# Top-2 gating scale: the second group's loads move to the scalar queue, in four parts

## The chip, the cores and the metric

The kernel runs on one core of a Trainium2 chip. The metric is the device time of one execution in microseconds (us).

## The reference

For 16 x 1024 = 16,384 tokens of 512 floats, `x` holds the tokens and `router_logits` eight logits a token. The two largest of the eight softmax probabilities are divided by their sum, and the token is written out twice, once scaled by each:

```python
probs = np.exp(router_logits - logits_max)
probs = probs / np.sum(probs, axis=-1, keepdims=True)
topk_indices = np.argsort(probs, axis=-1)[..., -k:]
topk_probs = np.take_along_axis(probs, topk_indices, axis=-1)
topk_probs = topk_probs / np.sum(topk_probs, axis=-1, keepdims=True)
x_expanded = x[:, :, np.newaxis, :].repeat(k, axis=2)
return (x_expanded * topk_probs[..., np.newaxis])
```

So 34 MB are read and 67 MB are written, and the arithmetic is one multiplication for each output element.

## The kernel before

Each of the 128 partitions handles 128 tokens ("rows"), in two groups of 65 and 63. A row is 2 KB when it is loaded and 4 KB when it is stored. The buffer `xs` has room for 65 loaded rows, `osp` for 18 output rows (of 4 KB), `WA` holds the two weights of every row.

The first group's rows are loaded in three transfers on the sync queue (6, 28 and 31 rows; line 120). The logits follow the first of them (lines 125 and 126), and `top2_weights` works out all weights: maxima and minima on VectorE, two sigmoids on ScalarE.

Then each of nine blocks is multiplied on VectorE (line 133), from `xs` into either `osp` or a part of `xs` whose rows have been used up, and stored by one transfer (line 145). The blocks, called stores 1 to 9, have 3, 15, 16, 15 and 16 rows in the first group and 16, 16, 15 and 16 in the second. Store 1 is issued on the scalar queue, all others on the sync queue. Two blocks that go into `osp` again (stores 4 and 8) are multiplied in two pieces: the first 3 (or 2) rows early, the others when an earlier store has left that part of `osp`.

The second group's rows come in three loads (16, 16 and 31 rows) that are issued on the sync queue behind store 5. The first two go into rows of `xs` that held store 3's output, the third into rows that held store 5's output, so they wait until those stores have landed.

All transfers of one queue are worked off in the order in which they are issued. Each engine's instructions, and each queue's issues, run in the order of the program; the waits between engines follow from the buffers' rows.

Of the kernel before, what the change touches and what calls it, by code (L numbers as in the profile page):

```python
# [1 line left out]

# [4 lines left out]

F32 = mybir.dt.float32
ALU = mybir.AluOpType
ACTF = mybir.ActivationFunctionType  # L10
P = 128


def top2_weights(nc, WA, dlt, room, logits, E):

    tt = nc.vector.tensor_tensor
    hi, lo, n = None, None, E  # L20
    while n > 1:
        n //= 2
        if hi is None:
            a, b = logits[:, :, 0:n], logits[:, :, n : 2 * n]
            nhi, nlo = room(n), b
            tt(nhi, a, b, op=ALU.max)  # L26
            tt(nlo, a, b, op=ALU.min)  # L27
        else:
            a, b = hi[:, :, 0:n], hi[:, :, n : 2 * n]
            nhi, nlo, tmp = room(n), room(n), room(n)  # L30
            tt(tmp, lo[:, :, 0:n], lo[:, :, n : 2 * n], op=ALU.max)  # L31
            tt(nlo, a, b, op=ALU.min)  # L32
            tt(nlo, nlo, tmp, op=ALU.max)  # L33
            tt(nhi, a, b, op=ALU.max)  # L34
        hi, lo = nhi, nlo
    tt(dlt, hi[:, :, 0], lo[:, :, 0], op=ALU.subtract)  # L36
    nc.scalar.activation(WA[:, :, 0], dlt, ACTF.Sigmoid, scale=-1.0)  # L37
    nc.scalar.activation(WA[:, :, 1], dlt, ACTF.Sigmoid, scale=1.0)  # L38

GROUPS = [65, 63]

LOADS = [[6, 28, 31], [16, 16, 31]]
BASE = [0, 1]

STORES = [
    [(0, 3, "osp", 0), (3, 15, "osp", 3), (18, 16, "xs", 0), (34, 15, "osp", 0), (49, 16, "xs", 33)],
    [(0, 16, "osp", 2), (16, 16, "xs", 0), (32, 15, "osp", 0), (47, 16, "xs", 32)],
]  # L50

L = 18

FREE = [3, 2]


@with_exitstack
def kernel(
    ctx: ExitStack,
    tc: tile.TileContext,  # L60
    x: bass.AP,
    router_logits: bass.AP,
    k: bass.AP,
    out: bass.AP,
):
    nc = tc.nc
    B, S, D = x.shape
    E = router_logits.shape[-1]
    N = B * S
    assert int(k) == 2 and E == 8 and N == P * sum(GROUPS)  # L70
    M = N // P

    x_v, o_v, rl_v = [], [], []
    t0 = 0
    for n in GROUPS:
        t1 = t0 + P * n
        x_v.append(
            x.rearrange("b s d -> (b s) d")[t0:t1].rearrange("(p m) d -> p m d", p=P)
        )
        o_v.append(  # L80
            out.rearrange("b s k d -> (b s) k d")[t0:t1].rearrange(
                "(p m) k d -> p m k d", p=P
            )
        )
        rl_v.append(
            router_logits.rearrange("b s e -> (b s) e")[t0:t1].rearrange(
                "(p m) e -> p m e", p=P
            )
        )
        t0 = t1  # L90

    wpool = ctx.enter_context(tc.tile_pool(name="wpool", bufs=1))
    xs = wpool.tile([P, max(GROUPS), D], F32)
    osp = wpool.tile([P, L, 2, D], F32)
    WA = wpool.tile([P, M, 2], F32)
    dlt = wpool.tile([P, M], F32)


    flat = osp.rearrange("p l k d -> p (l k d)")
    taken = [0]  # L100

    def room(n):
        o = taken[0]
        taken[0] += M * n
        return flat[:, o : o + M * n].rearrange("p (m n) -> p m n", n=n)

    logits = room(E)

    def place(where, at, n):

        if where == "osp":
            return osp[:, at : at + n]
        return xs[:, at : at + 2 * n, :].rearrange("p (r k) d -> p r k d", k=2)

    m0 = 0
    for g, G in enumerate(GROUPS):
        x0, r = BASE[g], 0
        for n in LOADS[g]:
            tc.keep_in_program_order(
                nc.sync.dma_start(xs[:, x0 + r : x0 + r + n, :], x_v[g][:, r : r + n, :])  # L120
            )
            r += n
            if g == 0 and r == 6:
                n0 = GROUPS[0]
                tc.keep_in_program_order(nc.sync.dma_start(logits[:, :n0], rl_v[0]))  # L125
                tc.keep_in_program_order(nc.sync.dma_start(logits[:, n0:], rl_v[1]))  # L126
                top2_weights(nc, WA, dlt, room, logits, E)
        assert r == G
        for r, n, where, at in STORES[g]:
            og = place(where, at, n)  # L130
            again = where == "osp" and at == 0 and r > 0
            for a, b in [(0, FREE[g]), (FREE[g], n)] if again else [(0, n)]:
                nc.vector.tensor_tensor(  # L133
                    og[:, a:b],
                    xs[:, x0 + r + a : x0 + r + b, :]
                    .unsqueeze(2)
                    .to_broadcast([P, b - a, 2, D]),
                    WA[:, m0 + r + a : m0 + r + b, :]
                    .unsqueeze(3)
                    .to_broadcast([P, b - a, 2, D]),  # L140
                    op=ALU.mult,
                )

            queue = nc.scalar if g == r == 0 else nc.sync
            tc.keep_in_program_order(queue.dma_start(o_v[g][:, r : r + n], og))  # L145
        m0 += G


# [1 line left out]
_INS = ['x', 'router_logits', 'k']  # L150
_OUTS = [((16, 1024, 2, 512), 'float32')]

_NUMBERS = {'k': 2}


# [26 lines left out]
```

## Time and profile before

| | |
|---|---|
| median of 3 runs | 239.9 us (239.83 to 239.99) |
| the profiled execution | 239.92 us |
| its span in the profile | 238.1 us |
| VectorE busy | 141.9 us (60% of the span) |
| ScalarE busy | 1.8 us |
| DMA | 101.19 MB in 2448 packets, mean 425 GB/s |

The span is what the profile shows between the first and the last instruction; the execution's own time is 1.8 us longer. An instruction that issues a transfer (SPq for the sync queue, ACTq for the scalar queue) takes 0.3 to 0.5 us, and the transfer runs on the 16 DMA engines after that. "To landing" is the time from the issue to the moment at which all 16 engines have reported the transfer complete; it holds the time for which the transfer stood behind others.

### The profile page before, as it was taken

What the parts mean: (1) busy time and instruction counts of PE and PEld (TensorE: products, weight loads), DVE (VectorE), ACT (ScalarE), POOL (GpSimd) and SP (SyncE); (2) the same over time, 40 slices, a digit from 0 to 9 for tenths busy, and PEclk for the clock granted to TensorE, in tenths of its full rate; (3) what the DMA queues carried; (4) which work ended last, traced back from release to release, by engine and by line L of the source; (5) the groups of instructions that cost most, each with busy time, mean ns of one, the idle gap of its engine ahead of it and who ended that gap; (6) DMA issues with size and microseconds to landing.
All of it is one profiled execution on the core that took longest, in us unless ns stands there. A gap on an engine that the chain in (4) does not pass through costs nothing.

```text
span 238.1 us, 102 instructions
## 1 busy us (share of the span) xinstructions
DVE 141.9 (60%) x22; ACT 1.8 (1%) x3; POOL 0.2 (0%) x4
## 2 busy tenths in 40 slices
DVE  0650499999699999100000699999406999950000
ACT  2000000000000000000000000000000000000000
POOL 0000000000000000000000000000000000000000
DMA  7979998979999999989899999898989999989894
GB/s 265 550 337 500 430 418 374 506 330 495 429 429 407 473 423 402 495 352 528 352 440 435 435 446 501 352 495 374 506 374 462 418 407 451 475 351 517 352 528 176
DMA packets 2448, 101.19 MB, mean 425 GB/s; under 512 B 272, under 2 KB 400, under 8 KB 528
## 3 DMA queue, kind: packets, MB, share of 16 engines
q1 hardware_dynamic: 2304, 99.62, 97.2%
q10 hardware_dynamic: 144, 1.57, 1.5%
HBM read 34.08 MB, written 67.11 MB: 425 GB/s over the span
## 4 chain that ended last, share of the span: by engine, by line
DMA 48%; DVE 40%; SPq 1%; issue 0%; DVEq 0%
DMA xs<-in_x_dram 26%; DVE osp L133 25%; DMA out_dram<-osp 22%; DVE xs L133 14%; SPq L125 0%; SPq L126 0%; SPq L120 0%; SPq L145 0%; DVEq L133 0%
## 5 line engine op out<-in xcount | busy, mean ns | idle before, releaser
L133 DVE TENSOR_TENSOR osp<-xs,WA 128x3072 f32<-128x3072 f32 (+5 forms) x7 | 69.4, 9908 | 61.6 <-DMA xs<-in_x_dram 47.5
L133 DVE TENSOR_TENSOR xs<-xs,WA 128x16384 f32<-128x16384 f32 x4 | 68.9, 17224 | 0.1
L26 DVE TENSOR_TENSOR osp<-osp 128x512 f32<-128x512 f32 x1 | 0.7, 692 | 8.1 <-DMA osp<-in_router_logits_dram 8.1
L37 ACT ACT_TABLE_LOAD x1 | 1.3, 1283 | 0.7 <-PEq L163 0.7
L27 DVE TENSOR_TENSOR osp<-osp 128x512 f32<-128x512 f32 x1 | 0.7, 691 | 0.0
L34 DVE TENSOR_TENSOR osp<-osp 128x256 f32<-128x256 f32 (+1 forms) x2 | 0.7, 352 | 0.0
L32 DVE TENSOR_TENSOR osp<-osp 128x256 f32<-128x256 f32 (+1 forms) x2 | 0.7, 352 | 0.0
L31 DVE TENSOR_TENSOR osp<-osp 128x256 f32<-128x256 f32 (+1 forms) x2 | 0.7, 352 | 0.0
L33 DVE TENSOR_TENSOR osp<-osp 128x256 f32<-128x256 f32 (+1 forms) x2 | 0.7, 351 | 0.0
L37 ACT ACTIVATE WA<-dlt 128x128 f32<-128x128 f32 x1 | 0.3, 314 | 10.1 <-DVE dlt L36 10.1
L36 DVE TENSOR_TENSOR dlt<-osp 128x128 f32<-128x128 f32 x1 | 0.3, 291 | 0.0
L38 ACT ACTIVATE WA<-dlt 128x128 f32<-128x128 f32 x1 | 0.3, 298 | 0.0
L163 POOL MEMSET const-bfloat16-1.0<- 128x1 bf16 x1 | 0.1, 101 | 0.0
L163 POOL MEMSET const-uint8-127<- 128x1 uint8 x1 | 0.1, 101 | 0.0
L163 POOL MEMSET const-float32-0.0<- 128x1 f32 x1 | 0.1, 98 | 0.2 <-issue 0.2
L163 POOL MEMSET const-float32-1.0<- 128x1 f32 x1 | 0.1, 98 | 0.0
## 6 DMA issues: line engine op xcount, KB each, us to landing
out_dram<-osp SPq DMA_DIRECT2D x3, 7680.0 KB, 23.4
xs<-in_x_dram SPq DMA_DIRECT2D x2, 7936.0 KB, 41.7
xs<-in_x_dram SPq DMA_DIRECT2D x2, 4096.0 KB, 40.4
xs<-in_x_dram SPq DMA_DIRECT2D x1, 7168.0 KB, 24.8
xs<-in_x_dram SPq DMA_DIRECT2D x1, 1536.0 KB, 6.0
out_dram<-osp ACTq DMA_DIRECT2D x1, 1536.0 KB, 24.8
osp<-in_router_logits_dram SPq DMA_DIRECT2D x1, 260.0 KB, 6.2
osp<-in_router_logits_dram SPq DMA_DIRECT2D x1, 252.0 KB, 6.4
```

The lines of the kernel that those rows point to most:

```text
L26: tt(nhi, a, b, op=ALU.max)
L27: tt(nlo, a, b, op=ALU.min)
L31: tt(tmp, lo[:, :, 0:n], lo[:, :, n : 2 * n], op=ALU.max)
L32: tt(nlo, a, b, op=ALU.min)
L33: tt(nlo, nlo, tmp, op=ALU.max)
L34: tt(nhi, a, b, op=ALU.max)
L36: tt(dlt, hi[:, :, 0], lo[:, :, 0], op=ALU.subtract)
L37: nc.scalar.activation(WA[:, :, 0], dlt, ACTF.Sigmoid, scale=-1.0)
L38: nc.scalar.activation(WA[:, :, 1], dlt, ACTF.Sigmoid, scale=1.0)
L133: nc.vector.tensor_tensor(og[:, a:b], xs[:, x0 + r + a : x0 + r + b, :] .unsqueeze(2) .to_broadcast([P, b - a, 2, D]), WA[:, m0 + r + a : ...
L163: nc = _bacc.Bacc("TRN2", target_bir_lowering=False, num_devices=1)
```

## The change

The second group's loads become four (16, 16, 16 and 15 rows) and are all issued on the scalar queue. They use two halves of `xs` in turn: rows 0 to 15 for loads 1 and 3, rows 16 to 31 (to 30) for loads 2 and 4. Ahead of load 1 ScalarE copies 2 rows of `xs` onto themselves (`PAUSE`), which waits for store 3 as load 1 does. Loads 3 and 4 wait until VectorE has multiplied the rows of loads 1 and 2.

The second group's blocks have 16, 16, 16 and 15 rows and match the loads one by one. They go to `osp` rows 0 to 15, to `xs` rows 33 to 64, to `osp` again and to `xs` rows 1 to 30. None of them is multiplied in pieces. The stores are issued on the sync queue, which issues no second-group load any more. The first group is as before.

```diff
-LOADS = [[6, 28, 31], [16, 16, 31]]
-BASE = [0, 1]
+LOADS = [6, 28, 31]
+LATE = [(16, 0), (16, 16), (16, 0), (15, 16)]
...
-    [(0, 16, "osp", 2), (16, 16, "xs", 0), (32, 15, "osp", 0), (47, 16, "xs", 32)],
+    [(0, 16, "osp", 0), (16, 16, "xs", 33), (32, 16, "osp", 0), (48, 15, "xs", 1)],
...
-FREE = [3, 2]
+FREE = 3
+PAUSE = 2
...
+    rows = xs[:, LATE[0][1] : LATE[0][1] + PAUSE, :]
+    tc.keep_in_program_order(nc.scalar.activation(rows, rows, ACTF.Copy))
+    first = [sum(n for n, _ in LATE[:i]) for i in range(len(LATE))]
+    def late(i):
+        load(nc.scalar, LATE[i][1], 1, first[i], LATE[i][0])
+    late(0)
+    late(1)
+    for i, (r, n, where, to) in enumerate(STORES[1]):
+        og = expand(n0, r, LATE[i][1], n, where, to, [0, n])
+        if i + 2 < len(LATE):
+            late(i + 2)
+        store(nc.sync, 1, r, n, og)
```

`expand` holds the multiplication of line 133, `load` and `store` the issues of lines 120 and 145, as they were.

## The prediction

> **What bounds the kernel now.** Stores are numbered 1 to 5 (first group) and 6 to 9, the second group's new loads 1 to 4. I read the page's DMA parts first, because every engine but VectorE is nearly empty, then the windows view, the chain of waits, the queues' own waits and the packet records (start, length, queue and size of each packet).
>
> ```profile
> span 238.1 us, 102 instructions
> ...
> DMA packets 2448, 101.19 MB, mean 425 GB/s; under 512 B 272, under 2 KB 400, under 8 KB 528
> ...
> q1 hardware_dynamic: 2304, 99.62, 97.2%
> q10 hardware_dynamic: 144, 1.57, 1.5%
> ```
>
> q1 is the sync queue, q10 the scalar queue. 97.2% + 1.5% = 98.7% of the span is 235.1 us of full work for all 16 DMA engines. The windows view (columns: stretch, length, DVE, ACT, POOL, clock, DMA share, GB/s) shows where the missing 1.3% lies:
>
> ```profile
> 4.00:236.90 232.90, 141.91 (x22) 0.51 (x2) 0.00 (x0) 1.00 1.00 431
> 0.00:1.70 1.70, 0.00 (x0) 0.98 (x1) 0.20 (x4) 1.00 0.00 0
> 236.90:238.10 1.20, 0.00 (x0) 0.00 (x0) 0.00 (x0) 1.00 0.00 0
> ```
>
> From 4.0 us to the last byte at 236.9 the share is 1.00: the engines never run dry. VectorE is busy 142 us of 238, and its waits cost nothing as long as the queue in front of the DMA engines holds work. So the chain of waits, which puts DVE and DMA pieces in turn, must not be read as what sets the time:
>
> ```profile
> 43.09 22.91 DMA out_dram<-osp
> 66.00 0.02 issue
> 66.03 12.97 DVE osp L133
> 79.00 0.02 issue
> 79.02 17.24 DVE xs L133
> 96.26 0.02 issue
> 96.27 0.33 SPq L145
> 96.61 0.05 issue
> 96.66 36.05 DMA xs<-in_x_dram
> ...
> 132.79 17.24 DVE osp L133
> 150.03 0.02 issue
> 150.05 30.49 DMA out_dram<-osp
> ```
>
> The 22.91 and 36.05 us are queueing. By the packet records the store issued at 43.09 starts its first packet at 47.1, right behind the packets ahead of it: a lead of 4.0 us, the smallest of all. The last store is issued at 211.87 and starts at 216.9. Each transfer gives each engine 8 data packets (128 partitions, one packet a partition) and one for the semaphore: 144 = 16 x 9. Lengths are constant: 2.42 us for 64 KB (a 16-row store), 2.27 for 60 KB, 1.21 for 32 KB (a 16-row load), so 1.14 for 30 KB by proportion. That is 27.1 GB/s an engine in loads and stores alike.
>
> **How two queues share.** One transfer in this trace used the scalar queue: the first store, 12 KB packets of 0.46 us beside 56 and 62 KB loads. The DMA view cut to three stretches (packets, MB, share):
>
> ```profile
> q10 hardware_dynamic: 16, 0.20, 41.8%
> q1 hardware_dynamic: 3, 0.17, 36.4%
> ```
>
> is 19.5 to 20.6 us: one scalar-queue packet on each of 16 engines. From 20.6 to 22.5 only sync-queue packets start (13), from 22.5 to 23.3 again 16 of q10. So the queues alternate strictly, packet by packet, and by the records a semaphore packet takes a turn too. That is why this 1.5 MB store, issued at 16.00, needed 24.8 us to land. In the shared stretch the packets keep their lengths, but for one stall of 0.39 us, in the packets that ended the 28-row load.
>
> **The change, part by part.**
>
> *Bytes.* The same 101.19 MB; one load more (31 rows become 16 + 15), 9 packets an engine of nearly unchanged total length: under 0.05 us. As the engines are full from 4.0 to 236.9, there is nothing to win; the change can only keep them full or not.
>
> *Sync queue.* Three load issues (0.4 us each) leave it, and with them the wait of the third for store 5, issued at 96.27 (24.3 us). Nothing was behind that wait until 150.05, so its removal is worth 0. Store 8's multiply is no longer cut in two (2 of its rows ran early, 2.28 us), so those 2 rows run after the wait; VectorE has room for them, since store 7 is still moving then.
>
> *Scalar queue.* The Copy on 2 rows waits for store 3 (issued 60.35, 25.0 to landing: 85.35). Behind it in the queue are only the four loads. This trace has no 1024-element ACTIVATE: one of 128 elements took 0.31, so 0.3 below and 8 x 0.31 = 2.5 above. I take 1.1 (two of 128 elements start 0.22 us apart, so most of the 0.31 grows with the elements, but not all). The Trainium skill's page "ScalarE: Activation LUTs", section "What ACT_TABLE_LOAD costs", prices it at 186 ns + 0.833 ns an element, an estimate of 1.04 us, which would leave the sum as it is. Load 1 is issued at 86.47.
>
> *First turn of the scalar queue.* Store 4 starts its packets at 84.6 to 85.1 (spread over engines) and then every 2.27: 86.9, 89.1, 91.4. The scalar store issued at 16.00 did not get the turns at 17.7 to 18.2 and got those at 20.1 to 20.5, so a turn lies more than 2.2 and less than 4.1 us after the issue. The first packet of the program came 1.0 after its issue on idle engines; 17.0 was before 17.7, so I read it as a turn settled one packet ahead. Then load 1, known at 87.5, misses 89.1 (settled 86.9) and starts at 91.4 to 91.9.
>
> *From there to the last load.* The scalar queue now holds work without a gap: loads 1 and 2 at once, load 3 is issued when VectorE has read load 1 (about 135, with load 2 not done before 147), load 4 about 164 (load 3 not done before 176). Each packet waits for one turn of the sync queue, which is never empty. 24 x 1.21 + 8 x 1.14 = 38.2 of loads. Between them 35 turns of sync: 5 packets of 2.27 left of store 4, 8 each of stores 5, 6, 7 and 2 of store 8 at 2.42 (26 x 2.42 = 62.9), and 4 semaphores: 74.3. Load 4 ends at 91.9 + 38.2 + 74.3 = 204.4 and lands 0.4 later (the last store's bytes ended at 236.9, its semaphore came at 237.3): 204.8.
>
> *The end.* The last store needs 15 rows on VectorE (16.16 us, the row of 128x15360): issued 221.0, first packet 1.0 later, 222.0. All other bytes are done at 236.9 - 8 x 2.27 = 218.7. So the engines stand dry for 3.3 us before the last store; before, that store was issued 5 us ahead of its turn. The loads are late because they get one turn in two with packets half as long, a third of the bandwidth, where a load used to have all of it. This is the cover that goes.
>
> *Unknown extras.* A cold start stretched the program's first packets by 0.5 us on the mean; stores may show 0 to 0.5, I take 0.1. A stall at a sync transfer's end with both queues active: 0.39 seen once, 0 elsewhere; four such ends, 0 to 1.6, I take 0.2. Nothing below 0: the lengths' minimum is their median.
>
> Sum: 3.3 + 0.1 + 0.2 = +3.6. The profiled execution took 239.92 (span 238.1 + 1.8), the median is 239.9, so 243.5.
>
> One rule speaks about this change as a whole. The row is the share of 1.00 at 431 GB/s. The Trainium skill, "DMA: Bandwidth & Descriptors", section "Issuing engines are not separate DMA queues", says that transfers issued from several engines interleave on the same 16 DMA engines, and a second issuer saves only issue time. The trace agrees; by the rule alone the time would stay 239.9, since it says nothing of which transfer then comes late.
>
> **Rivals.**
>
> *Earlier first turn (22%).* If a turn is not settled ahead and 2.7 us after the issue is enough, load 1 starts at 89.1 to 89.6. The interval 2.2 to 4.1 allows it. Loads 38.2, sync turns 6 x 2.27 + 25 x 2.42 = 74.1: load 4 lands 202.3, last store at 219.5, dry 0.8, with the extras 1.1: 241.0.
>
> *No slower (9%).* The queues alternate by whole transfers rather than by packets. Then store 4 ends at 102.7, load 1 lands near 113, load 4 near 200, and the last store is ready at 217, before 218.7: dry 0, 239.9. It decides at load 4's landing: 218.7 - 1.0 - 16.2 = 201.5. Against it stands the 16-packet alternation above. The Trainium skill's same page, "Queues, rings and completion order", has an engine draining a packet of some 9 to 17 descriptors before it changes rows. That would be a whole transfer here; the trace disagrees, with one partition row a turn.
>
> *Sharing costs rate (7%).* 17 to 40.2 us, with both queues active, moved 425 GB/s against 431 overall: 1.4% less. Over 112 us that is 1.6 more: 245.1, up to 246 with the stalls.
>
> *Forecast (62%).* 243.5, from 242.8 to 245.
>
> **Numbers.** 0.2% is 0.5 us, about what a measurement of this kernel can tell from no change. Slower: forecast, sharing, and nearly all of the early turn, 0.89. Same: the no-slower case and a little of the early turn, 0.09; faster 0.02, as no packet can shrink. The range leaves out the no-slower case: 240.4 to 245.8.
>
> **What the changed profile would show.** Right: a q10 share near 17% (16.5 MB + 1.6); the first scalar load packets at 91 to 92; load 4 landing near 205; the last multiply ending near 221, later than 218; a DMA hole of 3 us at about 219 in the slices; stores 4 and 5 landing some 7 and 17 us later than before. Wrong: a share of 1.00 up to the end; load 4 landing by 201.5; load packets starting back to back instead of one in two.

## The result and the profile after

The changed kernel takes 248.2 us (median of 6 executions, 247.3 to 255.2), the kernel before 240.0: a ratio of 1.0346, interval 1.0314 to 1.0377. Forecast were 243.5 and a range up to 245.8. The direction was right, the size less than half of what was lost. The profiled execution took 248.19, its span 246.4, 8.3 us more than before. Ratios leave out executions far above a kernel's fastest; single executions are given below where their scatter is the finding, and the profiles of the runs e3, f1 and m1 are of such slow ones.

The page after, the lines of the DMA queues:

```profile
span 246.4 us, 109 instructions
...
DMA packets 2592, 101.19 MB, mean 411 GB/s; under 512 B 288, under 2 KB 416, under 8 KB 544
...
q1 hardware_dynamic: 1872, 83.10, 78.5%
q10 hardware_dynamic: 720, 18.09, 17.1%
```

The bytes are the same; 78.5% + 17.1% = 95.6% of the span is 235.6 us of full work, as before (235.1). So no packet work was added to speak of: the engines stood still. The windows view of the profile after (length, DVE, ACT, POOL, clock, DMA share, GB/s) says where:

```profile
4.00:216.00 212.00, 131.94 (x21) 1.57 (x3) 0.00 (x0) 1.00 1.01 434
218.20:226.80 8.60, 7.70 (x1) 0.00 (x0) 0.00 (x0) 1.00 0.05 22
226.80:245.10 18.30, 0.00 (x0) 0.00 (x0) 0.00 (x0) 1.00 0.99 426
```

Full until 216; from 218.2 on, 8.6 us at a share of 0.05, and then the last store. The timeline after shows what that store waited for:

```profile
118.30 17.22 DVE L122 TENSOR_TENSOR osp<-xs,WA 128x16384 f32<-128x16384 f32 x1 [22.06 <-DMA xs<-in_x_dram]
149.97 17.22 DVE L122 TENSOR_TENSOR xs<-xs,WA 128x16384 f32<-128x16384 f32 x1 [14.44 <-DMA xs<-in_x_dram]
179.29 17.23 DVE L122 TENSOR_TENSOR osp<-xs,WA 128x16384 f32<-128x16384 f32 x1 [12.10 <-DMA xs<-in_x_dram]
209.74 16.16 DVE L122 TENSOR_TENSOR xs<-xs,WA 128x15360 f32<-128x15360 f32 x1 [13.22 <-DMA xs<-in_x_dram]
225.96 0.33 SPq L138 DMA_DIRECT2D out_dram<-xs  x1
```

Every second-group multiplication waits for its load, and each landing is the start time less about 0.1. The last multiplication ends at 225.9; by the packet records, which list each packet's start, length, queue and size, all other stores had run out by 218.4 on 14 engines, by 219.3 on another and only at 223.8 on the last. The forecast's place and mechanism are there, with 8.6 us where 3.3 were forecast.

The packet records show the rest. They carry no engine number, so I chained packets by each one's end and the next one's start; only the engine that runs apart is certain. Fifteen engines lose roughly 1 to 2.3 us in lengthened packets (packets longer than the usual time for their size) over the whole execution; before, each lost roughly 1 to 2, most of it in the first 26 us. One engine loses over 6, of it 5.4 after 100 us; in that time 14 others lose at most 0.3 each and one 1.1. Starts of its packets (S: sync, A: scalar, size in KB), and of an engine that stays level:

```
late   128.69 S64  131.26 A32  132.47 S64  135.31 A32  136.90 S64  139.34 A32  141.77 A32  143.49 S64
level  128.21 S64  130.63 A32  131.84 S64  134.25 A32  135.46 S64  137.88 A32  139.09 A32  140.30 S64
```

0.5 us behind at 128.7, 3.2 at the end of the row. It gains nothing back and ends store 8 at 223.8, some 5.5 after most others. A transfer has landed when its last engine reports, so the spread of the 16 reports is the price: 0.6 us for load 1, 3.3 for load 2, 8.4 for load 3, 10.3 for load 4.

### The profile page after: what moved, and what is told of

It is laid out like the page before. It is cut to its first block, busy times and chain, and to the rows that moved or that the text cites. A ratio compares the mean times of both kernels' runs of the same rounds, so it can differ in the third digit from the quotient of the medians.

```text
span 246.4 us, 109 instructions
## 1 busy us (share of the span) xinstructions
DVE 141.8 (58%) x21; ACT 2.9 (1%) x4; POOL 0.2 (0%) x4
## 2 busy tenths in 40 slices
DMA packets 2592, 101.19 MB, mean 411 GB/s; under 512 B 288, under 2 KB 416, under 8 KB 544
## 3 DMA queue, kind: packets, MB, share of 16 engines
q1 hardware_dynamic: 1872, 83.10, 78.5%
q10 hardware_dynamic: 720, 18.09, 17.1%
## 4 chain that ended last, share of the span: by engine, by line
DMA 50%; DVE 34%; another core or an unknown queue 6%; SPq 0%; ACT 0%; issue 0%; DVEq 0%; ACTq 0%
DMA xs<-in_x_dram 40%; DVE xs L122 21%; DVE osp L122 14%; DMA out_dram<-xs 10%; ACT xs L159 0%; SPq L145 0%; SPq L146 0%; SPq L134 0%; DVEq L122 0%; ACTq L159 0%
## 5 line engine op out<-in xcount | busy, mean ns | idle before, releaser
L122 DVE TENSOR_TENSOR osp<-xs,WA 128x3072 f32<-128x3072 f32 (+3 forms) x6 | 70.3, 11712 | 48.1 <-DMA xs<-in_x_dram 45.0
L122 DVE TENSOR_TENSOR xs<-xs,WA 128x16384 f32<-128x16384 f32 (+1 forms) x4 | 67.8, 16958 | 27.7 <-DMA xs<-in_x_dram 27.7
L159 ACT ACTIVATE xs<-xs 128x1024 f32<-128x1024 f32 x1 | 1.1, 1056 | 72.9 <-DMA out_dram<-xs 72.9
```

Of the source, the lines that this page charges most:

```text
L122: nc.vector.tensor_tensor(og[:, a:b], xs[:, x0 + a : x0 + b, :].unsqueeze(2).to_broadcast([P, b - a, 2, D]), WA[:, at + first + a : at + f ...
L159: tc.keep_in_program_order(nc.scalar.activation(rows, rows, ACTF.Copy))
```

## Experiments

All edits are to the changed kernel unless said, and are shown shortened. "Level" means that the 16 reports of each transfer lie within about 1 us; of an execution that was not profiled it is inferred from its time.

**Equal turns (e1).**

```diff
+        cuts = [0, n // 2, n] if g == 1 or r >= 34 else [0, n]
+        for a, b in zip(cuts, cuts[1:]):
+            queue.dma_start(o_v[g][:, r + a : r + b], og[:, a:b])
```

> The changed kernel, but each store from store 4 on is issued as two transfers of half the rows, so that a turn of the sync queue is 30 or 32 KB, as long as a load's packet. Theory A (two queues alternate packet by packet, and while both hold work one of the 16 engines falls behind the others by some 6 us; loads land late for both reasons, and the last store finds the engines dry): the loads now get half of the turns' time and load 4 lands near 185 to 195, no dry spell is left before the last store; what remains is the slow engine alone, seen as a spread of several us between the engines' last reports: 241 to 245 us. Theory B (alternation alone made the loads late, the slow engine is an accident of the profiled execution): 240.1 us, spread below 0.7 us at the end. Theory C (loads and stores that mix lose rate on all engines): above 245 us, all engines late alike.

Measured: 241.83 us, ratio 1.0072 (1.0049 to 1.0096). The last multiplication starts at 192.18, straight after the one before it, so load 4 was there in time: its last report came at 191.3, against 209.7 in the changed kernel. The windows of this run:

```profile
190.00:236.50 46.50, 18.31 (x2) 0.00 (x0) 0.00 (x0) 1.00 0.99 428
236.50:239.40 2.90, 0.00 (x0) 0.00 (x0) 0.00 (x0) 1.00 0.06 23
```

There is no dry spell; 15 engines end by 236.9, one at 239.4, and its reports come 2.8 us after the others' in every transfer that lands after 192. That is theory A, and 6.4 of the 8.2 us are gone: the length of a turn sets the loads' landing. One engine's lateness is smaller too (2.8 us against 5.5), so not all of the 6.4 is the turns' doing.

**The queue alone (e2).** The kernel before, its three second-group loads on the scalar queue:

```diff
-                nc.sync.dma_start(xs[:, x0 + r : x0 + r + n, :], x_v[g][:, r : r + n, :])
+                (nc.sync if g == 0 else nc.scalar).dma_start(xs[:, x0 + r : x0 + r + n, :], x_v[g][:, r : r + n, :])
```

> The kernel before, with one edit: the second group's three loads (16, 16, 31 rows) are issued on the scalar queue. Worked out with equal engines and strict turns, load 3 lands near 183 and the engines stand dry for about 1 us before store 8: 240.7 us (theory B). With one engine that falls behind while both queues hold work (theory A): 243 to 246 us, landings of the second group's loads spread by 2 us and more over the engines. If the two queues by themselves cost nothing: 239.9 us.

Measured: 245.64 us (243.3 to 247.2), ratio 1.0198 (1.0146 to 1.0250). The third load lands at 188.3 (equal engines: 183), its 16 reports 3.6 us apart; load 2's reports are 3.0 apart. The engines run short before store 8:

```profile
197.50:206.00 8.50, 8.47 (x2) 0.00 (x0) 0.00 (x0) 1.00 0.36 154
```

So the queue by itself, without new buffers or a fourth load, brings both costs.

**One queue (e6).** The changed kernel's loads on the sync queue:

```diff
-        load(nc.scalar, LATE[i][1], 1, first[i], LATE[i][0])
+        load(nc.sync, LATE[i][1], 1, first[i], LATE[i][0])
```

> The changed kernel's buffers and four loads, but issued on the sync queue in the same places of the program: one queue, no turns to share. Load 3 must wait for the multiply of load 1's rows and stands alone behind load 2 in the queue. Equal engines: load 2 lands near 142, the engines are dry from 141 to 151, one spell and no second: 249 us. All theories say so; theory A adds that the spread over the engines stays below 1 us, where the changed kernel's reached 10.

Measured: 251.68 us, one dry spell, and reports at most 1.0 us apart:

```profile
142.00:152.00 10.00, 10.00 (x2) 0.00 (x0) 0.00 (x0) 1.00 0.18 52
```

The change needed the second queue, because its loads 3 and 4 reuse rows that are multiplied late. Of the 2.7 us beyond the expectation, about 2 are lengthened packets, 1.5 to 2.9 on every engine; the rest is not traced.

**The Copy (e3).** Left out:

```diff
-    tc.keep_in_program_order(nc.scalar.activation(rows, rows, ACTF.Copy))
```

> The changed kernel without the Copy: load 1 is issued at about 85.4 instead of 86.5. If a turn is settled one packet ahead, as the prediction read it, load 1 is known at 86.4, in time for the turn that is settled at 86.9: its first packet starts at 89.1 instead of 91.3, and all loads after it come 2.4 us earlier. Equal engines: 240.7 us. With one slow engine (theory A): 1 to 3 us faster than the changed kernel's 248.2, so 245 to 247. If the first turn does not move, 248.2.

The first turn did not move: load 1 was issued at 85.47 instead of 86.51, and the stretch 89.0 to 91.0 again holds 16 packets of q1 alone, 91.0 to 91.9 again 16 of q10:

```profile
q1 hardware_dynamic: 16, 0.98, 113.3%
q10 hardware_dynamic: 16, 0.52, 134.8%
```

Load 1 landed at 118.2 in both. So the Copy cost nothing, and a first turn comes later than I read: the turns at 89.1 to 89.5, 3.6 to 4.1 us after this issue, were missed on all 16 engines. The store issued at 16.00 before had got those from 20.07 on, 4.1 us after it; in e2, with load 1 issued at 85.53, one engine got its turn at 89.42 and the other 15 missed theirs. The delay on busy engines is about 4 us, not the same on each. Whether a turn is settled a packet ahead stays open. Executions: 243.0 to 251.4, as scattered as those of the changed kernel; the ratio, 1.0185 (1.012 to 1.025), is that of the fastest of them.

**No wait for load 4 (e5, f2).** The last multiplication is gone:

```diff
-        og = expand(n0, r, LATE[i][1], n, where, to, [0, n])
+        og = expand(n0, r, LATE[i][1], n, where, to, [0, n]) if i < 3 else place("osp", 0, n)
```

> The changed kernel, but the last multiplication is left out and the last store sends the buffer of store 8 once more, so that it waits for no load; load 4 still runs and nobody reads it. Theory A: no dry spell is left, and what remains over 239.9 is the lateness of the one slow engine itself, 3 to 6 us: 242.5 to 246. Theory B (no slow engine, all of the loss is the dry spell): 239.9 to 240.2. If the time stays near 248, the dry spell was not what set the end.

Measured: 240.06 median of 10 executions, ratio 1.0000 (0.9989 to 1.0012). Six lie between 239.71 and 240.12, the other four at 244.2, 244.7, 245.1 and 248.3. The profiled one (239.80) is level, all reports within 0.6 us, and gives the landings that the forecast had worked out for equal engines:

| landing | forecast | level (e5) | changed kernel |
|---|---|---|---|
| load 1 | | 118.1 | 118.2 |
| load 2 | about 147 | 147.2 | 149.9 |
| load 3 | about 176 | 176.2 | 179.2 |
| load 4 | 204.8 | 204.6 | 209.7 |

Its timeline has the multiplications that follow loads 1 to 3:

```profile
118.25 17.23 DVE L122 TENSOR_TENSOR osp<-xs,WA 128x16384 f32<-128x16384 f32 x1 [21.98 <-DMA xs<-in_x_dram]
147.23 17.23 DVE L122 TENSOR_TENSOR xs<-xs,WA 128x16384 f32<-128x16384 f32 x1 [11.76 <-DMA xs<-in_x_dram]
176.24 17.22 DVE L122 TENSOR_TENSOR osp<-xs,WA 128x16384 f32<-128x16384 f32 x1 [11.79 <-DMA xs<-in_x_dram]
```

and its window is full from end to end:

```profile
4.00:236.70 232.70, 125.69 (x20) 1.57 (x3) 0.00 (x0) 1.00 1.00 432
```

So two queues cost no rate in themselves, theory C is out, and whether an engine is late differs from execution to execution. The executions of this kernel that are not level take 3 to 8 us longer (e5, f2), and f2's profile shows that without a dry spell: the DMA share is 1.00 up to 236.7, and three engines end 2.5 to 5.3 us after the middle of the 16.

**The last block in two pieces (e7).** 8 and 7 rows:

```diff
+        for a, b in ((0, 8), (8, n)) if i == 3 else ((0, n),):
+            og = expand(n0, r + a, LATE[i][1] + a, b - a, where, to + 2 * a, [0, b - a])
...
+            store(nc.sync, 1, r + a, b - a, og)
```

> The changed kernel, but the last block (15 rows) is multiplied and stored in two pieces of 8 and 7 rows, so that its first store is ready 8.7 us after load 4 has landed and not 16.2. With equal engines load 4 lands at 204.7, the first piece is issued at 213.4, before 218.7: no dry spell, 239.9 to 240.2. With one late engine and a landing near 210: issued at 218.4, hardly dry; what remains is that engine's own lateness of 2 to 6 us, 242 to 246. If the time stays at 248, the wait of the last multiplication for load 4 was not what set the end.

Measured: 239.97 once, the other five 242.4 to 246.4 (median of all 243.84; too scattered for a ratio), against 249.73 for the changed kernel on the same chip (e4, below). The profiled execution was level up to load 3, then one engine fell back; load 4 landed at 207.1, the first piece was ready before its turn:

```profile
207.12 16.35 DVE L122 TENSOR_TENSOR xs<-xs,WA 128x8192 f32<-128x8192 f32 x2 [13.52 <-DMA xs<-in_x_dram]
215.87 7.96 SPq L138 DMA_DIRECT2D out_dram<-xs  x2
```

No dry spell is left, and 2.9 us of the one engine's lateness at the end. With e5 this shows that the wait for load 4 set the changed kernel's end. This version at its best equals the kernel before and does not beat it.

**The changed kernel again (e4, f1), beside f2.**

> The changed kernel itself, unaltered, to see how its time spreads from execution to execution. The run with the free last store has shown both kinds: six executions within 0.5 us of 239.9, and four from 244 to 248; its profiled execution had all engines level and load 4 landing at 204.6. With that landing the forecast's sum (equal engines) gives 243.2 to 243.5 for the changed kernel. Theory A': executions without a late engine come out at 243.2 to 243.5 and none below 243; those with one at 245 to 256. Theory B': the time is 247 to 249 in all of them, so the late engine has nothing to do with chance and the sum is off by itself.

> The changed kernel once more, beside the next run on the same chip. Up to store 8's issue both run the same instructions. If an engine falls behind by chance in some executions, as 4 of 10 of the run with the free last store did, then some executions here come out at 243.2 to 243.5. If none does again and those of the next run are level again, chance is not enough: something that differs between the two programs decides it.

> The changed kernel without the last multiplication; the last store sends the buffer of store 8 once more. Chance alone: again between a third and two thirds of the executions within 0.5 us of 239.9, the others 242 to 249. If the chip decides: nearly all level or nearly all late, as the changed kernel beside it.

e4: 247.2 to 255.0, median 249.73, ratio 1.0307 (1.0291 to 1.0323); no time is that of level engines, which fits A' with an engine late in every execution and not B', which had 247 to 249 in all. Its profile has two late engines, both some 4.5 us behind at store 8's end. f1: 243.08, 246.3, 248.6, 249.5, 251.7 and 253.3; its ratio of 1.019 (1.0133 to 1.0247) is that of its fastest executions. So, with the six of the result, 1 of 18 executions came out at the forecast's level time, 243.1, and 17 from 246.3 up (e3, with the same turns, had one at 243.0 among four). f2 beside it: 242.9 to 248.4, none level, where the same program on the same chip was level in 6 of 10 in e5. So neither the program nor the chip alone decides it, and chance that is independent from execution to execution fits badly. What decides it was not found.

**Loads beside stores without any multiplication (m1, m6, m8; m2, m4, m5, m7).** Core of m1, m2, m6 and m8: eight loads on queue LQ and eight stores of a constant buffer on SQ, no waits between them. m4, m5 and m7 differ as their expectations say.

```
for g, r, n in parts:
    LQ.dma_start(xs[:, r : r + n, :], x_v[g][:, r : r + n, :])
    SQ.dma_start(o_v[g][:, r : r + n], osp[:, 0:n])
```

> No multiplication: eight loads (16 rows each, 17 and 15 at the groups' ends) on the scalar queue and eight stores of a constant buffer with as many rows on the sync queue, none waiting for the other; the output is the constant. Both queues hold work for some 210 us. Theory A: one engine falls behind more and more, the spread of the landings grows from 0.5 to 5 us and more, and the end comes later by as much than on one queue. Theory B: spread below 0.7 us throughout, last byte near 237. Theory C: spread small, end late by more than 2 us on all engines.

> The eight loads on the scalar queue beside the eight stores of a constant buffer on the sync queue once more (no multiplication, the output is the constant), on the chip of the other runs of this call: 240 to 265 us, one engine late by up to 25 us. If no engine is late here, the lateness belongs to single executions or chips.

> Loads on the scalar queue beside stores of a constant buffer on the sync queue (no multiplication, the output is the constant), for comparison on the same chip: 248 to 265 us, one engine late by 7 us and more.

Loads on the scalar queue, stores on the sync queue: 264.9 and 249.3 us (m1), 249.2 and 249.0 (m6), 249.3 and 249.1 (m8). The spread grows to 28 us in m1's profile (at 136 us; 23 at the end) and to 7.8 in m6 and m8; it is one engine in m1, one in m6 up to 134 us, and four in m8. In m1 most engines have ended by 242 and the last runs to 261.9. So neither VectorE nor the waits are needed for it.

> The eight loads alternately on the sync and the scalar queue, then the eight stores of a constant buffer alternately on both; no multiplication, the output is the constant. Two queues hold work nearly all the time, but loads meet loads and stores meet stores. If two busy queues make an engine fall behind, the spread of the landings grows here as it did in the two-queue run of loads beside stores (23 us there). If it takes loads and stores side by side on one engine, the spread stays below 1 us and the packets keep their lengths.

m4: 239.02 us. Both queues busy, packets in strict alternation, the spread never above 1.0:

```profile
24.00:236.00 212.00, 0.00 (x0) 0.00 (x0) 1.00 1.00 430
```

So two busy queues by themselves are not the cause; it takes loads beside stores. Even here nearly all lengthened packets (0.5 to 1.3 us an engine) lie at 77 to 81 us, where the last loads meet the first stores.

> The same loads and stores of a constant buffer, in the same order, all on the sync queue; the output is the constant. All theories: spread of the landings below 0.7 us throughout; last byte near 237 plus what the filling of the buffer costs at the start.

m2: 251.46, of which 8 us are a dry spell at the start, while the buffer is filled. Its packets are lengthened too, on all engines (3 to 6 us each), and the spread grows to 2.7 us: the expectation of 0.7 was wrong. Loads and stores that follow one another on one queue also disturb each other, but leave the engines nearly level.

> The same loads beside stores (no multiplication, the output is the constant), each store cut into two of half the rows, so that packets of both queues have the same length of 32 KB. If it takes unequal packets to bring one engine out of step with the others, no engine falls behind here: spread below 1.5 us. If loads beside stores on one engine are enough, the spread grows as in the run with unequal packets of this call.

m5: 243.95 and 241.82 us, spread 4.6, against 7.8 in m6 on the same chip. Unequal packets are not needed; with equal ones it was less, in one profile of each.

> Loads beside stores on two queues as in the earlier run, but each load is replaced by a copy of as many bytes from one buffer of the core's own memory to another, so that the stores to DRAM are met by nothing that reads DRAM; no multiplication, the output is the constant. If DRAM reads beside DRAM writes put engines behind, the packets keep their lengths and the spread of the landings stays below 1.5 us; if two unlike streams on one engine do, the spread grows to 5 us and more.

m7: 299.75 us. A 32 KB copy inside the core's memory takes 1.82 us instead of 1.21, so it can't be compared in time. No single packet is lengthened by over 0.2 us beyond its usual length (up to 1.2 in m8), yet the spread grows to 7 us: copies of one size differ throughout (1.66 to 1.96 us for 32 KB). Whether it takes DRAM reads beside DRAM writes is not settled by it.

## Why the prediction was wrong, step by step

- **Nothing to win.** Right: 101.19 MB, the level run full from end to end, and no execution of a changed version below 239.7 (but m4, which reads no logits and multiplies nothing).
- **The first turn.** Forecast 91.4 to 91.9, measured 91.3 to 91.8. Right by luck: the reading behind it (known 1.0 after the issue, settled one packet ahead) fell with e3, and with it the forecast's price of the Copy, whose 1.06 us (forecast 1.1) moved nothing.
- **The ring of turns, 38.2 + 74.3 us.** Right for level engines: load 4 lands at 204.6 in e5, forecast 204.8.
- **The end, 3.3 us.** Right as a mechanism, and in size for level engines. With e5's landing the changed kernel would end 5.1 us earlier than it did (209.7 less 204.6), at 243.1, an estimate; the fastest of its 18 executions took 243.1, though it was not profiled. Forecast 243.5.
- **Unknown extras, 0.1 + 0.2, and "lands 0.4 later".** This is the step that failed: the sum has no term for one engine falling behind the others. The cold start measured 0.04 us (2.31 instead of 2.27), and the stall at a transfer's end showed nowhere on all engines, only on single ones. But I took the spread over the engines, 0.3 to 0.7 us in every landing of before, as a constant, and looked for a loss that all engines share. The rows of before could not show the other kind: there the two queues met for 20 us only, with eight packets of 0.46 us an engine on one side. With one engine behind, load 4 landed at 209.7 instead of 204.8 (4.9 us), and 3.3 + 4.9 is the measured 8.2 with nothing left over.
- **Where the 4.9 come from.** The late engine lost over 5 us more than most others in lengthened packets. As load 2 landed 2.7 us late by it, store 7 was issued at 167.2 and not 164.5, when the sync queue had run empty (168 to 170), and the other engines used the free turns for loads; load 4's reports begin at 199.4, not 204.1. The late engine was still at store 6 and got none. So the spread of load 4 is 10.3 us while the engine is 5.5 behind.
- **Rival "sharing costs rate" (7%, 245.1 to 246).** Wrong as put: from 4 to 216 us the changed kernel moved 434 GB/s, the level run 435. What sharing costs is that the engines no longer stay level.
- **Rival "earlier first turn" (22%) and "no slower" (9%).** Neither occurred: the turn at 89.1 is out by e3, alternation by whole transfers by the packet records of every run, against the packet of 9 to 17 descriptors of the Trainium skill ("DMA: Bandwidth & Descriptors", "Queues, rings and completion order").
- **The rule that a second issuer saves only issue time** (the Trainium skill, "DMA: Bandwidth & Descriptors", "Issuing engines are not separate DMA queues"): m4 agrees, 430 GB/s on two queues against 431 before. The changed kernel shows what the rule leaves out: late loads and a late engine cost 3.5%.

**Open:** what makes an engine fall back. In the profiles of the changed kernel, e3 and e4 the late engine's first lengthened packet comes where two load packets follow one another, because a store's semaphore packet took the turn between them (110 us): it is 0.19 to 0.35 us longer, and packets of both queues are then lengthened again and again. But 0.18 in e5 led to nothing, and in e2, f1 and f2 an engine loses its first 0.1 to 0.2 us earlier, at 90 to 97 us, in a packet of store 4 between two loads, with no such pair.

One thing all of them share. In each of the eight profiles of the kernel with a late engine (changed, e1, e2, e3, e4, e7, f1, f2), the engine that loses most in lengthened packets up to 200 us is the one that started its first load packet on the scalar queue last of the 16 (in e4 the last two lose about as much): at 91.75 in the changed kernel, where the next one had started at 91.71, at 91.98 against 91.78 in f1. So which engine it is does not look like chance. Being last is not enough, since an engine is last in the level run too (91.79 against 91.77). In e2 the engine that got its first turn at 89.42, 2 us before the others, is lengthened from its very next packet on (0.22 us at 90.6). That an engine out of step with the others loses more, and so falls further back, fits all this; no run here forced one out of step to show it.

## What to carry to other kernels

Where the DMA engines are full from the first to the last byte, a second queue has nothing to win; it only decides whose bytes come first, in turns of one packet each and whatever the packets' lengths. Before a load is put beside stores, work out its landing with its share of the turns (here a third), and then look at what the last store needs after it; a last block in smaller pieces, or stores in packets as short as the loads', removes a dry spell (8.2 us lost became 1.7 in e1). And keep slack for the slowest of the 16 engines, not for their mean: loads beside stores let one or several fall back by 3 to 28 us, which the GB/s of a stretch does not show and the spread of a transfer's reports does.

## What was not expected of the hardware

- Single DMA engines fall behind the others of the 16 while loads and stores alternate on them: one in the changed kernel's profile (5.5 us), two in e4's, four in m8's (some 6 us), one in m1's (up to 28 us). Loads beside loads and stores beside stores on two queues stay within 1.0 us (m4).
- The engine that falls back most is the one that was last when the loads began, by 0.04 to 0.2 us, in all eight profiles of the kernel with a late engine.
- A transfer issued on an idle queue while the engines are busy with the other gets no turn for about 4 us after the issue: it got its first one after 4.1 us in the kernel before and missed those 3.6 to 4.1 us after it in e3. On idle engines the first packet came after 1.0 us.
- A 32 KB copy from the core's memory to itself takes an engine 1.82 us, a 32 KB load 1.21.
